# Scale alone on the way into the QKV projection; root and shift on the way out

## The chip, the core and the metric

The kernel runs on one core of a Trainium2 chip. A core has a matrix engine (TensorE, in the profile PE, with PEld for its weight loads), VectorE (DVE), ScalarE (ACT), GpSimd (POOL) and SyncE (SP), which issues the transfers. SBUF holds 128 partitions; PE writes its sums to PSUM. The metric is the device time of one execution in microseconds (us), from start to end.

## The reference

Two layers over 512 latent tokens and 256 context tokens of 1024 features: layer 0 mixes by grouped-query attention (16 query heads, 4 key and value heads of 64), layer 1 by a bidirectional state-space mixer, and each is followed by a gated convolutional feed-forward. All is float32. The change concerns the input of the attention:

```python
mod_l = jnp.split((silu_c @ ada_w[i] + ada_b[i])[:, None, :], 6, axis=-1)
mod_c = jnp.split(silu_cc @ ada_w[i] + ada_b[i], 6, axis=-1)
h_l = modulate(rms_norm(x, norm_mix_w[i]), mod_l[0], mod_l[1])   # x*rsqrt(mean x^2)*g*(1+scale)+shift
h_c = modulate(rms_norm(ctx, norm_mix_w[i]), mod_c[0], mod_c[1])
...
q_l, k_l, v_l = jnp.split(h_lat @ w_qkv, [Q_DIM, Q_DIM + KV_DIM], axis=-1)
q_l = rms_norm(q_l.reshape(bsz, seq, N_HEADS, HEAD_DIM), q_norm)
k_l = rms_norm(k_l.reshape(bsz, seq, N_KV_HEADS, HEAD_DIM), k_norm)
```

The root of a token is one number for the token; scale and shift are vectors over the features, one pair for all latents and one for the context.

## The kernel before

Data lies with features on the partitions: X holds eight tiles of 128 features x 768 tokens (512 latents, then 256 context). A float32 operand of a product is split into a rounded part and a remainder (`hi` and `lo`, `wh` and `wl`), and a product is the sum of three: hi by wh, lo by wh, hi by wl (`mm3`, L99 to L108). The casts (L85) run on ScalarE, the remainders (L87) on VectorE, in the opening also on GpSimd.

**The opening** is written out by hand in its order for PE, ScalarE and VectorE (`manual_schedule` in `attention`). SP's transfers are issued in the order of the program: first the latents of X (four loads of two feature tiles each), the parameters `par` (128 x 548), then per k-step m the weights of the modulation (`adaA`, 1 MB in three pieces), a slab of projection weights (`wslab`, 128 x 768: six groups of 128 columns) and, ahead of the rest of the slabs, the context.

1. ScalarE squares the eight latent tiles (L574), VectorE adds them up (L576), PE sums over the features (`ssa`, L274), and the root is made of it (`rstd_rows`, L265 on) and turned into a row over all partitions (`rsT`, L292). Meanwhile PE runs products of ones that nobody reads (`busy`, tile `warm`, L568).
2. SiLU of the condition (L584 on); `ada` makes the modulation of feature tile m: eight products (`ps_ada`, L128), a copy out of PSUM on VectorE (`ada_sb`, L130), two transposing products (`ps_adt`, L134), and `modulation` (L140 on), which adds the bias and makes `moda`, gain times (1 + scale).
3. `modulated` (L315) makes the operand of the products: VectorE multiplies X by `moda` and the root (`ht`, L321), ScalarE adds the shift and rounds (`hha`, L330), VectorE takes the remainder (L331).
4. Eight k-steps (m = 0 to 7): six groups of three 128x512 products into six PSUM sums (`ps_l`) kept open throughout. Beside them run the modulation and operands of the next step, in m = 1 and 2 the squares of the context (L615, L617), in m = 4 to 7 the operands of the context (`modulated` with `pool=True`, which leaves the remainder to GpSimd, L326 to L328).

**The rest of the projection** is ordered by the framework's scheduler, which respects marked orders. The six latent sums are copied to `raw` (L646); six groups of context sums `ps_c` follow (24 products of 128x256 each, copied at L863). `raw[0]` holds keys, `raw[1]` and on queries. `normed` (L668 on) makes the per-head norm and the rotary positions: squares (`qsq`, L671), gain (L672), four transfers that swap partitions (`qsw`, L675), sums on PE (`ssq`, L680), then VectorE and ScalarE up to the split into `qh` and `ql`. `values` (L654) makes six tiles of 128 tokens (24 products `ps_v` each, L660), four of latents and then two of context, and copies them out (L662). Then begins the loop over eight pairs of heads: the maxima of the scores (`ps_m`, reduced by VectorE at L768), the scores, the exponentials and the outputs. For pairs 4 to 7 the queries are projected inside this loop (`q_units`, L730 on; `ps_q`, copied by ScalarE at L738).

Of the kernel before, what the change touches and what calls it, by code (L numbers as in the profile page):

```python
# [7 lines left out]
P = 128  # L8
# [7 lines left out]
D = 1024  # L16
# [13 lines left out]
_n = 0  # L30
# [22 lines left out]
_col("cc", 2 * KT)  # L53
_col("qn", 1)
_col("kn", 1)
# [55 lines left out]
def ada(g, src, layer, chunks, m0, nm, big=True):  # L111


    nc = g.nc
    cols = nm * len(chunks) * P
    per = (1024 if big else T) // cols
    st = []
    for k0 in range(0, KT, per):
        n = min(per, KT - k0)
        t = t4(g, "wada") if big else t3(g, "wada")  # L120
        t = t[:, : n * cols].rearrange("p (k a b) -> p k a b", k=n, a=len(chunks))
        nc.sync.dma_start(t.rearrange("p k a b -> p (k a b)"), src[:, k0 * cols : (k0 + n) * cols])
        st += [t[:, k].rearrange("p a b -> p (a b)") for k in range(n)]
    yield 0
    ps = Bank(g, "ps_ada")
    for k in range(KT):
        j = k % 4
        nc.tensor.matmul(ps[32 * j : 32 * j + 32, 0:cols], g.sc32[:, k, :], st[k], start=k < 4, stop=k >= 4)  # L128
    sb = g.t3p.tile([P, 512], F32, tag="t2", bufs=6, name="ada_sb")
    nc.vector.tensor_copy(sb[:, 0:cols], ps[:, 0:cols])  # L130
    yield BREAK
    pt = Bank(g, "ps_adt")
    for i in range(cols // P):
        nc.tensor.matmul(pt[:, 2 * i : 2 * i + 2], sb[:, i * P : (i + 1) * P], g.sel, start=True, stop=True)  # L134
# [130 lines left out]
def rstd_rows(g, sq, n, cols, width, name, bank, behind=lambda: None):  # L265
# [17 lines left out]
    nc.vector.scalar_tensor_tensor(u, y, -0.5, u, ALU.mult, ALU.mult)  # L283
    rb = t3(g, f"rb{name}", n=n)
# [230 lines left out]
def attention(g, adas, project, X):  # L515
# [6 lines left out]
    g.h = [[htiles(g, n, f"a{i}_{m}") for m in range(KT)] for i, n in enumerate((L, C))]  # L522
    hl, hc = g.h
# [5 lines left out]
    mods = [ada(g, I["adaA"][m], 0, (0, 1), m, 1, big=False) for m in range(KT)]  # L529
# [12 lines left out]
    def slab():  # L542

        k = len(slabs)
        slabs.append(None)
        st = t4(g, "wst")[:, :W6]
        nc.sync.dma_start(st, I["wslab"][k])
        yield
        slabs[k] = hi, lo = slab_tile("wsh"), slab_tile("wsl")
        split(g, st, hi, lo, lo_engine="pool" if k < 7 else "dve")  # L550
# [19 lines left out]
    busy(38)  # L570
    acc = t3(g, "acc", n=L)
    for m in range(KT):
        sq = t2("sql") if m else acc
        nc.scalar.activation(sq, xs[0][m], AF.Square)  # L574
# [8 lines left out]
    e = g.p.tile([P, 2 * KT], F32, name="silu")  # L583
# [5 lines left out]
    next(norm)  # L589
# [7 lines left out]
    rs_ps, rsl = rsl, t3(g, "rsl", n=L)  # L597
    nc.scalar.copy(rsl, rs_ps)
# [7 lines left out]
    for m in range(KT):  # L606
        if 1 <= m < KT - 5 + 1:
            next(mods[m + 5 - 1])
            next(loads[m + 5 - 1])
        if m == 1:  # L610
            sqc = t3(g, "sqc", n=C)
        if m in (1, 2):
            for a in range(4 * m - 4, 4 * m):
                sq = t2("sqc")[:, :C] if a else sqc
                nc.scalar.activation(sq, xs[1][a], AF.Square)  # L615
                if a:
                    nc.vector.tensor_tensor(sqc, sqc, sq, ALU.add)  # L617
        if m == 3:
            norm = rstd_rows(g, sqc, C, g.ones[:, :1], D, "a", Bk)
            next(norm)  # L620
        if m == 4:
            rsc = t3(g, "rsc", n=C)
            pt, _, _ = next(norm)
            nc.scalar.copy(rsc, pt[:, :C])
        for j in range(6):
            if m + 1 < KT and j == 0:
                next(mods[m + 1])
            k_step(m, j, pl[j], hl)
            if m + 1 < KT:
                if j == 0:  # L630
                    next(loads[m + 1], None)
                if j == 0 + 1:
                    next(mods[m + 1])
                    modulated(g, hl[m + 1], xs[0], rsl, 0, L, 0, 1, 0, 0, m + 1)
            if m >= 4 and j == 1:
                for a in (2 * m - 8, 2 * m - 7):
                    modulated(g, hc[a], xs[1], rsc, 0, C, 0, 1, 0, 1, a, pool=True)
# [7 lines left out]
    for j in range(6):  # L645
        nc.scalar.copy(raw[j][:, :L], pl[j])  # L646
    wv = []
# [3 lines left out]

    def values():
        for t in range(T // P):
            h, c0 = (hl, t * P) if t < 4 else (hc, t * P - L)  # L654
# [7 lines left out]
            nc.scalar.copy(vt[t], ps[:, :256])  # L662
# [66 lines left out]

    def q_units(p):  # L730
        qraw[p] = qs = t3(g, "qs")
        for h, c0, n in ((hc, L, C), (hl, 0, L)):
# [5 lines left out]
            nc.scalar.copy(qs[:, c0 : c0 + n], ps[:, :n])  # L738
# [120 lines left out]
    for n, j in enumerate((0, 1, 2, 4, 5, 3)):  # L859
        ps = Bk("ps_c")  # L860
        for k in range(KT):
            k_step(k, j, ps[:, :C], hc)
        nc.scalar.copy(raw[j][:, L:], ps[:, :C])  # L863
        if n in (1, 3):
            wv.append(load_w(g, I["wv"][len(wv)], pin=True))
# [261 lines left out]
def ssd(g, x, norm, wf, close):  # L1127
# [331 lines left out]
    xn = [[g.p.tile([P, C], F32, tag="h256", bufs=16, name=f"x{m}{i}") for i in range(2)] for m in range(KT)]  # L1459
# [91 lines left out]
def body(nc, tc, I, out, dbg=None):  # L1551
# [181 lines left out]
```

## Time and profile before

| | |
|---|---|
| time of three executions | 1885.97, 1887.44, 1888.54 us; median 1887.44 us |
| the profiled execution | 1889.8 us, of it span 1888.0 us |
| TensorE clock granted, mean | 0.995 |
| instructions in the span | 27471 |
| ps_l, values and maxima begin at | 18.26, 89.19 and 96.31 us |

The profile is of one execution; the median is of others. A span runs from the first to the last instruction of the core. Engines work beside each other, so the busy times don't add up. The rows of a timeline begin with the start and the duration; a bracket at the end says how long the engine idled before and which instruction released it. The rows of groups give count, then busy time and mean nanoseconds of one, then idle time. Rows of the profile name a tile's write first and what it reads behind the arrow.

### The profile page before, as it was taken

Reading aid. Unit: us, or ns where it says so; the run is one execution under the profiler, and the core shown is the slowest. Engines: PE = TensorE matmul, PEld = TensorE weight load, DVE = VectorE, ACT = ScalarE, POOL = GpSimd, SP = SyncE. Lnnn points to the kernel's source line nnn. Section 1 sums busy time; section 2 is a strip of 40 time slices with the busy share of each in tenths; the row PEclk is TensorE's granted clock in tenths of the full one; section 3 lists DMA queues with packets and bytes.
Section 4 is the critical chain, followed back from the end, with each engine's and each line's share of the span. In section 5 each row is a group of like instructions: output and inputs, shape, how many; then the busy total and the mean of one; then the engine's idle time right before and its main releaser. Section 6 shows DMA issues by size and latency. Waiting matters only on the chain.

```text
span 1888.0 us, 27471 instructions
## 1 busy us (share of the span) xinstructions
PE 1862.3 (99%) x10794; PEld 1535.3 (81%) x10794; DVE 1346.3 (71%) x2013; ACT 832.8 (44%) x1422; POOL 251.8 (13%) x220
## 2 busy tenths in 40 slices
PE   9999999999999999999999999999999999999999
PEld 7865555689888888888898888888887888888887
DVE  5688899678777777444478977777888576565655
ACT  3655544354122222222256677766667352323331
POOL 2100000030000000000030435454434200000000
PEclk9999999989999999999999999999999999999999
DMA  9223241024443555222223344343344323323232
GB/s 342 68 83 114 89 145 62 2 78 145 156 124 121 171 188 167 68 68 67 80 77 106 91 123 133 104 133 123 108 129 136 97 74 105 101 83 107 90 101 90
DMA packets 73489, 210.02 MB, mean 111 GB/s; under 512 B 8976, under 2 KB 14480, under 8 KB 73232
## 3 DMA queue, kind: packets, MB, share of 16 engines
q1 hardware_dynamic: 73360, 208.26, 34.8%
q8 instruction: 85, 1.39, 0.3%
q14 instruction: 44, 0.36, 0.1%
HBM read 198.79 MB, written 6.82 MB: 109 GB/s over the span
## 4 chain that ended last, share of the span: by engine, by line
PE 84%; DVE 7%; DMA 3%; ACT 3%; issue 2%; SPq 1%; POOL 1%; DVEq 0%; POOLq 0%; ACTq 0%
PE ps_up L104 10%; PE ps_up L105 10%; PE ps_up L107 10%; PE ps_d L104 6%; PE ps_d L107 6%; PE ps_d L105 6%; PE ps_in L104 4%; PE ps_in L105 4%; PE ps_in L107 4%; PE ps_o L802 2%; PE ps_s L838 2%; PE ps_st L1348 1%; PE ps_wo L105 1%; PE ps_wo L107 1%; PE ps_wo L104 1%
## 5 line engine op out<-in xcount | busy, mean ns | idle before, releaser
L87 DVE TENSOR_TENSOR wl<-wst,wh 128x1024 fp32r<-128x1024 f32 x207 | 256.8, 1241 | 276.8 <-PE ps_up L105 114.2
L85 ACT CAST wh<-wst 128x1024 fp32r<-128x1024 f32 x207 | 216.9, 1048 | 440.6 <-DMA wst<-in_wup 319.5
L105 PE MATMUL ps_up<-hlf,wh 128*128 128x512 f32 x992 | 351.6, 354 | 0.0
L107 PE MATMUL ps_up<-hhf,wl 128*128 128x512 f32 x992 | 351.4, 354 | 0.0
L104 PE MATMUL ps_up<-hhf,wh 128*128 128x512 f32 x992 | 351.2, 355 | 0.0
L104 PEld LDWEIGHTS ps_up<-hhf,wh 128*128 128x128 f32 x992 | 187.5, 189 | 26.2
L105 PEld LDWEIGHTS ps_up<-hlf,wh 128*128 128x128 f32 x992 | 187.6, 189 | 26.1
L107 PEld LDWEIGHTS ps_up<-hhf,wl 128*128 128x128 f32 x992 | 187.4, 189 | 26.1
L104 PE MATMUL ps_in<-hhs,wh 128*128 128x512 f32 (+1 forms) x544 | 199.2, 366 | 0.5 <-ACT raw L1214 0.5
L107 PE MATMUL ps_in<-hhs,wl 128*128 128x512 f32 (+1 forms) x544 | 193.7, 356 | 0.0
L105 PE MATMUL ps_in<-hls,wh 128*128 128x512 f32 (+1 forms) x544 | 193.6, 356 | 0.0
L107 PE MATMUL ps_d<-hdh,wl 128*128 128x512 f32 (+1 forms) x496 | 173.4, 350 | 0.0
L104 PE MATMUL ps_d<-hdh,wh 128*128 128x512 f32 (+1 forms) x496 | 173.3, 350 | 0.1
L105 PE MATMUL ps_d<-hdl,wh 128*128 128x512 f32 (+1 forms) x496 | 172.9, 349 | 0.0
L1030 DVE SCALAR_TENSOR_TENSOR X<-ps_d,mod,X 128x256 f32<-128x256 f32 (+1 forms) x176 | 102.5, 612 | 27.1 <-PE ps_d L107 26.8
L104 PEld LDWEIGHTS ps_in<-hhs,wh 128*128 128x128 f32 x544 | 102.8, 189 | 15.3 <-issue 1.0
L107 PEld LDWEIGHTS ps_in<-hhs,wl 128*128 128x128 f32 x544 | 102.7, 189 | 14.8
L105 PEld LDWEIGHTS ps_in<-hls,wh 128*128 128x128 f32 x544 | 102.9, 189 | 13.0
L105 PEld LDWEIGHTS ps_d<-hdl,wh 128*128 128x128 f32 x496 | 93.2, 188 | 14.4 <-DVE hdl L87 0.2
L107 PEld LDWEIGHTS ps_d<-hdh,wl 128*128 128x128 f32 x496 | 93.2, 188 | 13.1
L104 PEld LDWEIGHTS ps_d<-hdh,wh 128*128 128x128 f32 x496 | 93.0, 188 | 12.9 <-ACT hdh L85 0.3
L167 DVE SCALAR_TENSOR_TENSOR junk<-wada,cb 128x1024 f32<-128x1024 f32 x80 | 97.2, 1215 | 1.0 <-ACT cb L158 0.8
(389 smaller groups left out, 3668.1 us busy)
## 6 DMA issues: line engine op xcount, KB each, us to landing
wst<-in_wup SPq DMA_DIRECT2D x88, 512.0 KB, 3.6
wada<-in_adaT SPq DMA_DIRECT2D x56, 512.0 KB, 3.6
wst<-in_win SPq DMA_DIRECT2D x48, 512.0 KB, 3.6
wst<-in_wdown SPq DMA_DIRECT2D x44, 512.0 KB, 3.7
E<-ad SPq DMA_DIRECT2D x64, 256.0 KB, 6.8
wada<-in_adaB SPq DMA_DIRECT2D x24, 512.0 KB, 4.6
ec<-ead SPq DMA_DIRECT2D x64, 128.0 KB, 4.3
wst<-in_wout SPq DMA_DIRECT2D x16, 512.0 KB, 3.6
```

Source lines behind the costliest of these rows:

```text
L85: keep(nc.scalar.copy(hi, src))
L87: keep(eng.tensor_tensor(lo, src, _r(hi), ALU.subtract))
L104: mm(out, wh, ah, start=first, stop=False)
L105: mm(out, wh, al, start=False, stop=False)
L107: i = mm(out, wl, ah, start=False, stop=last)
L167: g.tc.keep_in_program_order(nc.vector.scalar_tensor_tensor(junk, w, 1.0, cb[:, v * D : (v + 1) * D], ALU.mult, ALU.mult, accum_out=md[:, ...
L802: nc.tensor.matmul(po[S64[e], :n], v, pr[:, 512 * e + off : 512 * e + off + n], start=first, stop=last)
L838: nc.tensor.matmul(outs[e], a[S64[e], k], b[S64[e], q], start=i == 0, stop=False)
L1030: nc.vector.scalar_tensor_tensor(ap, o[:, c0:c1], gate[:, m, v : v + 1], ap, ALU.mult, ALU.add)
L1348: nc.tensor.matmul(ps[:, d * 256 : (d + 1) * 256], Bt[:, t * P : (t + 1) * P], xw[d][t], start=t == ts[0], stop=t == ts[-1])
```

## The change

The operand of a latent becomes x times `moda` alone. With r the root of a token, W the weights and s the shift, (x moda r + s) W = r (x moda W) + s W, so r is multiplied in when a sum is taken out of PSUM, and s W is added there. s W comes for keys and queries from two further columns of the context's operand tile (256 + 2 = 258 = `WX`), which hold the shift, split into hi and lo like the rest; for the values from a row `sv` that VectorE makes of the weights (`shift_row`) and that PE sums over the partitions by a product with ones (`ps_sv`). The context keeps its operands as they were. In detail:

- X comes in one load per k-step, behind the modulation's weights of the step, and no longer first of all; of `par`, the first 74 columns come behind the first piece of step 0's weights, the rest behind the last slab.
- The squares of the latents move from ahead of step 0 into steps 1 to 5, their sums and root into steps 6 and 7; the context's squares move to steps 2 and 3, its root to 4 and 5, its operands to 5, 6 and 7. Before the first latent product there are 14 + 2 + 6 warm products, not 38 + 8 + 3. Step 0 does first all groups' products hi by wh, then hi by wl, then lo by wh.
- The copies L646 and the latent half of L738 become VectorE multiplications by the root's row (`rsl`); a ScalarE bias and a two-column copy (`shift_col`) follow.
- The values are made in the order context, then latents; the latents' copies become VectorE operations with the root (`rsv`) and `sv`. The loaded weights of the values (`wvf`) are kept until `shift_row` has read them.
- hi and lo of a context operand lie in one tile of twice 258 columns. The same pool serves tiles of layer 1.

```diff
+    def scaled(m):
+        gain = g.moda[0][1][:, m, 0:1]
+        hi, lo = hr[m]
+        nc.scalar.activation(hi, xs[0][m], AF.Identity, scale=gain)
+        nc.vector.scalar_tensor_tensor(lo, xs[0][m], gain, _r(hi), ALU.mult, ALU.subtract)
...
-    busy(38)
-    acc = t3(g, "acc", n=L)
-    for m in range(KT):
-        sq = t2("sql") if m else acc
-        nc.scalar.activation(sq, xs[0][m], AF.Square)
-        if m:
-            nc.vector.tensor_tensor(acc, acc, sq, ALU.add)
-    norm = rstd_rows(g, acc, L, g.ones[:, :1], D, "a", Bk)
...
+    busy(14)
     next(mods[0])
-    busy(8)
-    rsl, _, _ = next(norm)
+    busy(2)
     next(mods[0])
     next(loads[0], None)
-    busy(3)
-    modulated(g, hl[0], xs[0], rsl, 0, L, 0, 1, 0, 0, 0)
+    scaled(0)
+    busy(6)
...
+    first_step(wh0, ah0, range(6), True)
+    next(mods[1])
+    next(loads[1], None)
+    first_step(wl0, ah0, range(4))
+    next(mods[1])
+    scaled(1)
+    shifts(0, 0)
+    first_step(wl0, ah0, range(4, 6))
+    first_step(wh0, al0, range(6))
...
+    lat = {1: (0, 1), 2: (2,), 3: (3,), 4: (4, 5), 5: (6, 7)}
...
     for j in range(6):
-        nc.scalar.copy(raw[j][:, :L], pl[j])
+        nc.vector.tensor_tensor(raw[j][:, :L], pl[j], rsl, ALU.mult)
...
+    def shift_row():
+        for k in range(KT):
+            w = wvf[k // 4][:, (k % 4) * 256 : (k % 4 + 1) * 256]
+            sh = g.mod[0][0][:, k, 0:1]
+            if k:
+                nc.vector.scalar_tensor_tensor(sv, w, sh, sv, ALU.mult, ALU.add)
+            else:
+                nc.vector.tensor_scalar(sv, w, sh, None, ALU.mult)
+
     def values():
-        for t in range(T // P):
+        for t in (4, 5, 0, 1, 2, 3):
...
+            if not t:
+                ps = Bk("ps_sv")
+                placed[0] = nc.tensor.matmul(ps[:, :256], g.ones, sv, start=True, stop=True)
+                nc.scalar.copy(sv, ps[:, :256])
...
-            nc.scalar.copy(vt[t], ps[:, :256])
+            if t < 4:
+                nc.vector.scalar_tensor_tensor(vt[t], ps[:, :256], rsv[:, t : t + 1], sv, ALU.mult, ALU.add)
+            else:
+                nc.scalar.copy(vt[t], ps[:, :256])
...
         for k in range(KT):
-            k_step(k, j, ps[:, :C], hc)
+            k_step(k, j, ps[:, :WX], hc)
         nc.scalar.copy(raw[j][:, L:], ps[:, :C])
+        nc.scalar.activation(raw[j][:, :L], raw[j][:, :L], AF.Identity, bias=shift_col(ps))
...
+        if n == 5:
+            shift_row()
```

What stands in a row on PE at the program's start, before (`ssa` are the latents' sums of squares, `rsTa` the root's row):

```order
L568 MATMUL warm<-ones 128x128 x38
L274 MATMUL ssa<-ones,acc 128x1 x4
L128 MATMUL ps_ada<-wada,sc_83 32x256 x8
L568 MATMUL warm<-ones 128x128 x8
L292 MATMUL rsTa<-cst,rba 128x128 x4
L134 MATMUL ps_adt<-cst,ada_sb 128x2 x2
L568 MATMUL warm<-ones 128x128 x3
L128 MATMUL ps_ada<-wada,sc_83 32x256 x8
L104 MATMUL ps_l<-hha_0_102,wsh 128x512
```

And after, with line numbers of the changed kernel (`hhr` and `hlr` are hi and lo of a latent operand):

```order
L590 MATMUL warm<-ones 128x128 x14
L134 MATMUL ps_ada<-wada,sc_78 32x256 x8
L590 MATMUL warm<-ones 128x128 x2
L140 MATMUL ps_adt<-cst,ada_sb 128x2 x2
L590 MATMUL warm<-ones 128x128 x6
L641 MATMUL ps_l<-hhr_97,wsh 128x512 x6
L134 MATMUL ps_ada<-wada,sc_78 32x256 x8
L641 MATMUL ps_l<-hhr_97,wsl 128x512 x4
L140 MATMUL ps_adt<-cst,ada_sb 128x2 x2
L641 MATMUL ps_l<-hhr_97,wsl 128x512 x2
L641 MATMUL ps_l<-hlr_98,wsh 128x512 x6
```

The latents' sums and root stand behind the first products now, and step 1's modulation has moved from ahead of the first product into step 0.

On VectorE, at the end of the first query and the first maxima, before (`raw_739` is the query of pair 0):

```order
L694 TENSOR_TENSOR raw_739<-raw_739,qy 128x768
L693 SCALAR_TENSOR_TENSOR qsq<-ssq,qsq 128x512
L693 SCALAR_TENSOR_TENSOR qsq<-ssq,qsq 128x256
L87 TENSOR_TENSOR wl<-wst,wh 128x1024
L695 SCALAR_TENSOR_TENSOR raw_739<-qsq,raw_739 128x768
L87 TENSOR_TENSOR ql<-raw_739,qh 128x768
L768 TENSOR_REDUCE ma<-ps_m 128x2x2
```

And after (`raw_711` is the same query):

```order
L769 TENSOR_TENSOR raw_711<-raw_711,qy 128x768
L768 SCALAR_TENSOR_TENSOR qsq<-ssq,qsq 128x512
L768 SCALAR_TENSOR_TENSOR qsq<-ssq,qsq 128x256
L770 SCALAR_TENSOR_TENSOR raw_711<-qsq,raw_711 128x768
L91 TENSOR_TENSOR ql<-raw_711,qh 128x768
L718 TENSOR_SCALAR sv<-wst,mod_81 128x256
L716 SCALAR_TENSOR_TENSOR sv<-wst,mod_81,sv 128x256 x7
L853 TENSOR_REDUCE ma<-ps_m 128x2x2
```

The eight operations of `shift_row` stand between the split of the query and the first reduction of the maxima.

On PE the values stood before as 60 products `ps_v` in a row with the first maxima behind them, and the rest of `ps_v` among these. After, where the context's two tiles end and the latents' begin:

```order
L732 MATMUL ps_v<-wl,hhc_120 128x256
L732 MATMUL ps_v<-wh,hhc_120 128x256
L725 MATMUL ps_sv<-sv,ones 128x256
L732 MATMUL ps_v<-wh,hhr_97 128x256
L732 MATMUL ps_v<-wl,hhr_97 128x256
L732 MATMUL ps_v<-wh,hlr_98 128x256
```

48 products `ps_v` stand ahead of `ps_sv` (`hhc` is a context operand), then 12 more, then the first maxima.

More of the change, by code (lines that the diff above doesn't have):

```diff
@@ L108, in mm3, with ada @@
     return i
[L111 removed]
+def ada(g, src, layer, chunks, m0, nm, big=True, also=lambda: None):
     nc = g.nc
@@ L528, in attention @@
     man.__enter__()
-    mods = [ada(g, I["adaA"][m], 0, (0, 1), m, 1, big=False) for m in range(KT)]
+    first_par = lambda: nc.sync.dma_start(g.par[:, :NFIRST], I["par"][:, :NFIRST])
+    mods = [ada(g, I["adaA"][m], 0, (0, 1), m, 1, big=False, also=(lambda: None) if m else first_par) for m in range(KT)]
     W6 = 6 * P
@@ L604, in k_step, with first_step @@
         mm3(g, tuple(w[:, ks] for w in slabs[m]), [(out, h[m])], m == 0, m == KT - 1)
[L606 to L620, printed above, removed]
+    (wh0, wl0), (ah0, al0) = slabs[0], hr[0]
+    def first_step(w, h, js, first=False):
+        for j in js:
+            nc.tensor.matmul(pl[j], w[:, j * P : (j + 1) * P], h, start=first, stop=False)
+    first_step(wh0, ah0, range(6), True)
[7 more added lines that the diff above has]
+    first_step(wh0, al0, range(6))
+    acc, sqc = t3(g, "acc", n=L), t3(g, "sqc", n=C)
+    rsv = g.p.tile([P, L // P], F32, tag="rsv", bufs=1, name="rsv")
+    lat = {1: (0, 1), 2: (2,), 3: (3,), 4: (4, 5), 5: (6, 7)}
+    rows = {}
+    for m in range(1, KT):
+        if m < 4:
+            begin(m + 4)
         if m == 4:
-            rsc = t3(g, "rsc", n=C)
-            pt, _, _ = next(norm)
-            nc.scalar.copy(rsc, pt[:, :C])
+            nc.sync.dma_start(g.par[:, NFIRST:], I["par"][:, NFIRST:])
         for j in range(6):
@@ L627, in attention @@
                 next(mods[m + 1])
[L628 to L632, printed above, removed]
-                    next(mods[m + 1])
[L634 to L637, printed above, removed]
+            k_step(m, j, pl[j], hr)
+            if m + 1 < KT and j == 0:
+                next(loads[m + 1], None)
+            if j == 1:
+                if m + 1 < KT:
+                    next(mods[m + 1])
+                    scaled(m + 1)
+                shifts(m - 1, 1)
+                shifts(m, 0)
+            if j == 2:
+                for a in lat.get(m, ()):
+                    squared(acc, xs[0][a], a)
+                if m in (2, 3):
+                    for a in range(4 * m - 8, 4 * m - 4):
+                        squared(sqc, xs[1][a], a)
+                if m == 4:
+                    rows["c"] = rstd_rows(g, sqc, C, g.ones[:, :1], D, "a", Bk)
+                    next(rows["c"])
+                if m == 5:
+                    rsc = t3(g, "rsc", n=C)
+                    nc.scalar.copy(rsc, next(rows["c"])[0][:, :C])
+                if m == 6:
+                    rows["l"] = rstd_rows(g, acc, L, g.ones[:, :1], D, "a", Bk, col=rsv)
+                    next(rows["l"])
+                if m == 7:
+                    rsl = t3(g, "rsl", n=L)
+                    nc.scalar.copy(rsl, next(rows["l"])[0])
+            if j == 3:
+                for a in {5: (0, 1), 6: (2, 3, 4), 7: (5, 6, 7)}.get(m, ()):
+                    modulated(g, tuple(t[:, :C] for t in hc[a]), xs[1], rsc, 0, C, 0, 1, 0, 1, a, pool=True)
+    shifts(KT - 1, 1)
     for _ in mods:
@@ L1456, in ssd @@
         prev = cur
-    xn = [[g.p.tile([P, C], F32, tag="h256", bufs=16, name=f"x{m}{i}") for i in range(2)] for m in range(KT)]
+    xn = [[t[:, :C], t[:, C : 2 * C]] for t in (g.p.tile([P, 2 * WX], F32, tag=f"h{C}", bufs=8, name=f"x{m}") for m in range(KT))]
     for m in range(KT):
```

100 lines of the change are left out of this document (69 added, 31 removed).

## The prediction

> **What bounds the kernel now.** First comes the page's table of busy times, then the chain of work that ended last, by engine.
>
> ```profile
> PE 1862.3 (99%) x10794; PEld 1535.3 (81%) x10794; DVE 1346.3 (71%) x2013; ACT 832.8 (44%) x1422; POOL 251.8 (13%) x220
> PE 84%; DVE 7%; DMA 3%; ACT 3%; issue 2%; SPq 1%; POOL 1%; DVEq 0%; POOLq 0%; ACTq 0%
> ```
>
> PE, the matrix engine, is the bound, and 16% of the chain lies elsewhere. The change edits the opening and the QKV projection, so the second view is the timeline of the first 100 us: where does PE wait, and for whom?
>
> ```profile
> 1.05 10.20 PE L568 MATMUL warm<-ones 128*128 128x128 f32 x76 [1.05 <-DVE ones L1575]
> 17.49 0.72 ACT L330 ACTIVATE hha<-ht,mod 128x512 fp32r<-128x512 f32 x1 [3.11 <-DVE ht L321]
> 18.26 0.50 PE L104 MATMUL ps_l<-hha,wsh 128*128 128x512 f32 x1 [0.28 <-ACT hha L330]
> 24.65 0.50 PE L104 MATMUL ps_l<-hha,wsh 128*128 128x512 f32 x1
> 34.00 0.61 PE L134 MATMUL ps_adt<-cst,ada_sb 128*128 128x2 f32 x4 [1.31 <-DVE ada_sb L130]
> 71.57 0.37 ACT L863 COPY raw<-ps_c 128x256 f32<-128x256 f32 x1
> 89.19 7.19 PE ps_v L660 x60
> 95.45 0.96 DVE L87 TENSOR_TENSOR ql<-raw,qh 128x768 fp32r<-128x768 f32 x1 [0.90 <-ACT qh L85]
> 96.31 0.50 PE L764 MATMUL ps_m<-kh,qh 64*128 64x256 f32 x4
> ```
>
> PE idles or makes warm products that compute nothing until 18.26, since the first latent operand needs squares, a root and the modulation. From there it hardly stops. The values (89.19) are followed by the maxima (96.31), whose query operand qh is ready less than 1 us before: the chain through the query of pair 0 has no slack. The table of windows gives the granted clock of some stretches.
>
> ```profile
> core 0: us, PE busy (x) PEld busy (x) DVE busy (x) ACT busy (x) POOL busy (x), PEclk, DMA share, GB/s
> 0.00:3.40 3.40, 2.35 (x11) 2.35 (x12) 0.45 (x3) 1.58 (x2) 0.20 (x4) 1.00 0.39 99
> 3.40:6.80 3.40, 3.40 (x29) 3.40 (x29) 0.85 (x2) 1.97 (x4) 0.00 (x0) 1.00 1.04 396
> 18.26:64.43 46.17, 43.91 (x264) 31.55 (x264) 25.33 (x59) 17.50 (x34) 13.97 (x10) 0.96 0.58 219
> 64.43:89.19 24.76, 23.86 (x173) 20.57 (x174) 13.95 (x20) 19.23 (x35) 2.98 (x4) 1.00 0.38 115
> 31.43:34.85 3.42, 2.11 (x12) 1.49 (x11) 2.62 (x5) 0.00 (x0) 1.83 (x1) 1.00 1.02 401
> 34.85:38.26 3.41, 3.41 (x10) 2.63 (x9) 1.69 (x4) 0.73 (x1) 0.00 (x0) 0.50 1.02 395
> 38.26:41.67 3.41, 3.41 (x30) 2.46 (x29) 1.24 (x5) 1.13 (x3) 0.81 (x1) 1.00 1.05 401
> 222.58:225.99 3.41, 2.65 (x16) 1.60 (x17) 3.41 (x4) 0.60 (x1) 0.00 (x0) 1.00 0.66 195
> 225.99:229.40 3.41, 3.41 (x15) 2.46 (x15) 2.24 (x4) 1.20 (x2) 0.00 (x0) 0.50 0.26 87
> 112.34:260.00 147.66, 143.10 (x899) 78.87 (x898) 128.37 (x180) 83.23 (x113) 0.00 (x0) 0.99 0.36 113
> ```
>
> The clock moves in steps of 3.41 us. After a window in which PE was busy for 2.11 or 2.65 us, the next runs at 0.50; the window at 34.85, wholly busy, is followed by 1.00. Half a clock is dear:
>
> ```profile
> 36.00 0.63 PE L105 MATMUL ps_l<-hla,wsh 128*128 128x512 f32 x1
> 36.43 0.63 PE L107 MATMUL ps_l<-hha,wsl 128*128 128x512 f32 x1
> 22.39 0.39 PE L105 MATMUL ps_l<-hla,wsh 128*128 128x512 f32 x1
> 22.62 0.40 PE L107 MATMUL ps_l<-hha,wsl 128*128 128x512 f32 x1
> ```
>
> Products start 0.43 us apart there, 0.23 at full rate: a slow stretch loses 0.20/0.43 = 0.46 of its length, 1.6 us for a window. One profiled execution (1889.8 us, 1888.0 of it span) carries all this; it stands 2.4 above the median 1887.44.
>
> **The change part by part.** *1. The first product.* Squares, root and shift leave its path. What remains: the first weights of the modulation, SiLU, one modulation product, its transposition, one ScalarE pass.
>
> ```profile
> 4.64 0.63 ACT L574 ACTIVATE acc<-X 128x512 f32<-128x512 f32 x1 [2.32 <-DMA X<-in_xT]
> 8.99 1.15 ACT L574 ACTIVATE sql<-X 128x512 f32<-128x512 f32 x2 [0.23 <-DMA X<-in_xT]
> 12.38 1.07 PE L128 MATMUL ps_ada<-wada,sc 128*32 128x256 f32 x16
> ```
>
> The four 512 KB loads of X end waits from 4.64 to 8.99: 1.45 us each, so the stream starts in effect at 3.2. The change loads 1.05 MB of modulation weights, parameters, 0.1 MB of constants, slab 0 (0.39 MB) and the first X (0.26 MB) in this order. At 2.8 us a MB the weights are in at 6.2 and X at some 8.2. The modulation product ends near 7.0; its PSUM copy, transposition and two VectorE steps bring me to 8.5; ScalarE's pass (0.72, as at 17.49) ends at 9.25. First product: **9.4** instead of 18.26. Between it and the second k-step lie the 6.39 us of before and one more modulation product (1.07), which stood ahead of 18.26 before: second step at 9.4 + 6.39 + 1.07 = 16.9, or 17.0 with a short wait for the second set of weights, against 24.65: **−7.65**. The spread squares cost nothing if ScalarE (17.50 of 46.17 us busy) and VectorE (25.33) hide them; uncovered, eight at 0.63 would be 5.0.
>
> *2. Waits of the k-steps.* The one at 34.00 comes of VectorE's PSUM copy standing behind four additions of squares:
>
> ```profile
> 30.18 3.43 DVE L617 TENSOR_TENSOR sqc<-sqc 128x256 f32<-128x256 f32 x4
> ```
>
> PE is idle for 46.17 − 43.91 = 2.26 us between 18.26 and 64.43 (1.31 of it here) and for 24.76 − 23.86 = 0.90 from there to the values. I let all of it go, since additions and context operands are spread and made earlier, and with the wait at 34.00 its window at half clock (1.6): −4.8. Added: the latents' sum of squares and transposed roots move into the run of products (1.0: the eight passes of L274 and four of L292 that stood before 18.26 took 1.05 and 0.60, partly beside each other); two copies of the modulation again stand behind additions (0.4, a third of 1.31); the first sum for the norm of the keys waits longer, since two bias passes, 2 × 0.59 by the L646 row below, and a small copy stand ahead of its square on ScalarE (1.4). −4.8 + 1.0 + 0.4 + 1.4 = −2.0. With part 1 the values start **9.6** earlier. Bounds: −4.9, if only part 1's gain holds and the 2.8 comes on top, and −12.4, if none of the 2.8 shows.
>
> *3. The shift's row.* It is the new wait. The values of latents t = 0 wait for ps_sv, a product of ones with sv, and sv is the last of eight dependent VectorE operations that stand behind ql on VectorE's order (shown above). Behind ps_sv on PE stand the 12 products of t = 0's first half and then the maxima, so nothing passes it.
>
> ```profile
> 73.89 2.51 SPq L675 DMA_DIRECT2D qsw<-raw  x4
> 94.59 0.83 ACT L85 CAST qh<-raw 128x768 fp32r<-128x768 f32 x1 [1.95 <-DVE raw L695]
> L321 DVE SCALAR_TENSOR_TENSOR ht<-X,moda,rsc 128x256 f32<-128x256 f32 x8 | 3.4, 479 | 0.0
> L646 ACT COPY raw<-ps_l 128x512 f32<-128x512 f32 x6 | 3.3, 590 | 0.0
> L813 DVE TENSOR_TENSOR o<-ps_o,y 128x512 f32<-128x512 f32 x8 | 5.5, 685 | 0.6 <-ACT y L812 0.5
> ```
>
> From the copy of the first context group (71.57) to the end of ql (96.41) it is 24.8 us before. Bias passes also stand ahead of the keys' transfers of qsw on the way there: +1.4 by the same price. The row itself is 8 × 0.48 = 3.8 (a dependent operation may take 0.63, as L617's do over a wait: 5.0). So sv is ready 30.0 after the copy. PE gets there after 89.19 − 71.57 = 17.6 us less 0.6 of waits that go, and 48 of 60 steps of the values, 0.8 × 7.19 = 5.8: 22.8. **+7.2**, bounds 5 and 9 by the sizes just named, and nothing at all if the row's rank on VectorE does not bind (rival 1). ps_sv itself is one full-precision product: between 0.13 (1.07/8) and 0.47 (four passes of 0.117, from 29 in 3.40); I take **0.4**.
>
> *4. The clock after it.* 7.2 us hold at least one wholly idle window. Then half rate lasts until a window was busy throughout: half a window on average and a whole one, 5.1 us at 0.46 = **+2.3**, bounds 1.6 and 3.1 (one window, two). The Trainium skill, "TensorE: Matmul & The Clock Gate", Part 1, has half rate after at least one idle window of about 3.4 us and full rate after a busy one. This trace agrees in the step (3.41 us), but by its rows a partly idle window is enough; for this wait both give the same 2.3.
>
> *5. Evacuations.* Six L646 copies go to VectorE with a factor (0.69 by L813 instead of 0.59) while PE is in ps_c, hidden. Four latent values become VectorE operations beside the maxima: **+0.4** on PE, bounds 0 and 2 (four of 0.48). In pairs 4 to 7 a query copy becomes a VectorE multiplication (0.69), a two-column copy (0.16 by a guess from the 128x4 copy below) and a ScalarE bias: VectorE gets 4 × 0.85 = 3.4 us more in a stretch where it is 128.37 of 147.66 busy.
>
> ```profile
> L772 DVE COPY mb<-ma 128x4 f32<-128x4 f32 x2 | 0.3, 165 | 0.0
> L104 PE MATMUL ps_first<-xa,wh 128*128 128x258 f32 x16 | 4.7, 292 | 0.0
> L104 PE MATMUL ps_first<-hhf,wh 128*128 128x256 f32 x40 | 11.4, 288 | 0.1
> ```
>
> I put a third of it on the path, **+1.3**; bounds 3.4, and −1.6 if the half window at 225.99 falls away. 258 columns instead of 256 cost 4 ns by these rows: nothing. The order of all engines after the attention is the same: nothing.
>
> Sum: −9.6 + 7.2 + 0.4 + 2.3 + 0.4 + 1.3 = **+2.0**: 1891.8 in a profiled execution, 1889.4 beside the median.
>
> **The rivals.** *1. The row is hidden.* The 24.8 us of the chain were measured with PE's sums for the norms and the transfers in between. If it gets 7 us shorter where these come earlier, wait and clock (9.5) vanish: −7.5, **1879.9**. For it: 1.95 and 0.90 us of waiting ahead of qh and ql alone. Against it: both rows name VectorE and ScalarE as releasers, not PE or a transfer.
> *2. VectorE bounds the pairs (slower).* The window at 222.58, with VectorE busy for 3.41 of 3.41 and PE for 2.65, shows how it goes: each further such window costs 1.6 of clock. If all 3.4 us come onto the path it is +2.1 on my sum, and if one window more tips, 1.6 on top: **1891.5 to 1893.1**. It decides from the point where VectorE has no idle time left around a pair; 87% on average speaks for a third rather than all.
> *3. The start stays cold.* Passes go 11 in the 2.35 us up to 3.40 and 29 in the next 3.40: the start is slow too. 14 warm products (28 passes) end at 5.65; then PE has products only in pieces until 9.4. By the rows, a window at 6.8 with some 80% of work (2.65 of 3.41 is 78%) is followed by half rate: 5.1 us at 0.46, +2.3, **1891.7**. By the skill's rule, which asks for a wholly idle window, this rival would not come about. I give it about an eighth, since the 80% is itself an estimate and lies at the edge.
> *4. The start doesn't move as said.* Transfers run at 396 GB/s already at 3.40; if the first set lands 3 us later, **1892.4**.
>
> **How the numbers follow.** Forecast 0.44, rival 1 0.21, rival 2 0.16, rival 3 0.13, rival 4 0.06. A measurement of this kernel tells 0.2%, 3.8 us, from no change: faster is under 1883.7, slower over 1891.2. The forecast's own spread is 1884 to 1894 (the −12.4 of part 2 and the 5 of part 3 on one side, 9, 3.1 and part 2's −4.9 on the other, never all at once): 0.03 faster, 0.33 same, 0.08 slower. Rival 1 is faster (0.20 of 0.21); rival 2 slower (0.14 of 0.16); rival 3 0.05 same, 0.08 slower; rival 4 slower (0.05 of 0.06). So 0.23, 0.42, 0.35. The range goes down to 1880, which leaves out half of rival 1, and up to 1894.5, which leaves out the most unfavourable sums: 0.18 outside.
>
> **What would show it.** The first latent product at 9 to 10 us and the second k-step at 17 (rival 4: 3 later). Granted clock 1.00 between 7 and 15 us (rival 3: 0.50). Values starting near 79. ps_sv idle before it by 5 to 9 us, released by sv's last operation, and the window behind it at 0.50 (rival 1: no idle time, clock 1.00). Between 112 and 260 the sum of PE's idle time and of half-clock windows as before or a window more (rival 2). I am wrong if ps_sv doesn't wait, or if the time after attention changes by more than 2 us.

## The result

The changed kernel takes 1899.62 us (median of six runs, 1896.67 to 1901.75) against 1887.36 us before (six runs, 1885.97 to 1888.54): a ratio of 1.0065, 95% interval 1.0052 to 1.0078. It is slower, and lies above the range of 1880 to 1894.5. The profiled execution took 1900.94 us with a span of 1899.1 us, 11.1 us more than the span of before; the forecast for this difference was +2.0.

The page of the changed kernel, its busy times and its chain by engine:

```profile
PE 1860.5 (98%) x10742; PEld 1530.3 (81%) x10742; DVE 1354.8 (71%) x2047; ACT 834.4 (44%) x1427; POOL 252.3 (13%) x219
PE 78%; DVE 10%; issue 4%; ACT 3%; DMA 3%; POOL 2%; SPq 0%; DVEq 0%; POOLq 0%; ACTq 0%
```

PE is busy for 1.8 us less than before, in a span that is 11.1 us longer: it idles for 12.9 us more, and VectorE's share of the chain grew from 7% to 10%. The timeline of PE, at the places that the prediction named:

```profile
10.68 1.65 PE L641 MATMUL ps_l<-hhr,wsh 128*128 128x512 f32 x6
17.71 0.50 PE L108 MATMUL ps_l<-hhr,wsh 128*128 128x512 f32 x1
39.42 0.61 PE L140 MATMUL ps_adt<-cst,ada_sb 128*128 128x2 f32 x4 [2.25 <-DVE ada_sb L136]
88.72 0.43 PE L732 MATMUL ps_v<-wh,hhc 128*128 128x256 f32 x1 [3.61 <-DVE wb L807]
99.43 1.22 PE L725 MATMUL ps_sv<-sv,ones 128*128 128x256 f32 x2 [3.28 <-DVE sv L716]
102.88 0.50 PE L849 MATMUL ps_m<-kh,qh 64*128 64x256 f32 x4
```

Set against the same points of before:

| begins (us) | before | after | difference |
|---|---|---|---|
| first latent product | 18.26 | 10.68 | −7.58 |
| second k-step | 24.65 | 17.71 | −6.94 |
| twelfth product of the context sums | 69.28 | 63.51 | −5.77 |
| values | 89.03 | 88.72 | −0.31 |
| first maxima | 96.31 | 102.88 | +6.57 |
| output projection, ps_dn | 378.44 | 384.79 | +6.35 |
| end of the span | 1888.0 | 1899.1 | +11.1 |

(Before, eleven products of the context sums stand among the last of the latents'; from the twelfth on the same work is done on both sides. The first product of the values begins at 89.03; the 89.19 given ahead of the prediction is the start of a piece of the chain.) So 7.3 of the 7.6 us won at the start are gone before the values, most of it in the context sums; the values lose 6.9; the loop over the pairs of heads is as long as before; and the stretch behind the attention, where hardly a line was edited, loses 4.7. The windows around the three long waits (2.25, 3.61 and 3.28 us), by the granted clock:

```profile
core 0: us, PE busy (x) PEld busy (x) DVE busy (x) ACT busy (x) POOL busy (x), PEclk, DMA share, GB/s
37.66:41.07 3.41, 1.65 (x12) 1.52 (x12) 2.10 (x5) 0.54 (x1) 1.09 (x1) 1.00 1.04 397
41.07:44.48 3.41, 3.41 (x9) 2.74 (x10) 2.52 (x8) 2.15 (x7) 0.00 (x0) 0.50 1.04 399
85.44:88.85 3.41, 0.13 (x1) 0.16 (x2) 3.32 (x7) 3.35 (x7) 0.00 (x0) 1.00 0.00 0
88.85:92.27 3.42, 3.42 (x17) 3.42 (x18) 3.39 (x5) 1.95 (x3) 0.00 (x0) 0.50 0.37 104
95.68:99.09 3.41, 0.47 (x5) 0.26 (x3) 3.16 (x8) 2.05 (x3) 0.00 (x0) 1.00 0.21 59
99.09:102.50 3.41, 3.07 (x12) 2.89 (x13) 0.29 (x1) 0.37 (x1) 0.00 (x0) 0.50 0.55 179
```

Each wait is followed by one window at half rate, some 1.6 us of loss each. Who lets PE wait is seen in VectorE's timeline:

```profile
35.61 3.42 DVE L621 TENSOR_TENSOR sqc<-sqc,sq 128x256 f32<-128x256 f32 x4
38.96 0.41 DVE L136 COPY ada_sb<-ps_ada 128x256 f32<-128x256 f32 x1
...
85.61 2.89 DVE L784 TENSOR_TENSOR kl<-raw,kh 64x768 fp32r<-64x768 f32 x3
88.42 0.21 DVE L807 COPY wb<-ps_c 128x2 f32<-128x2 f32 x2
...
94.50 0.96 DVE L91 TENSOR_TENSOR ql<-raw,qh 128x768 fp32r<-128x768 f32 x1 [1.82 <-ACT qh L89]
95.38 0.35 DVE L718 TENSOR_SCALAR sv<-wst,mod 128x256 f32<-128x256 f32 x1
95.77 3.61 DVE L716 SCALAR_TENSOR_TENSOR sv<-wst,mod,sv 128x256 f32<-128x256 f32 x7
```

At 39 the copy of the modulation out of PSUM stands behind four additions of the context's squares, as at 34 before (and behind one of the latents' at 35.01). At 88 two tiny copies (`wb`, the shift's columns of the last context sums) are the last readers of those sums' banks; they stand behind three remainders of the keys, and the first product of the values needs such a bank. At 95 the eight operations of the shift's row follow the query's split, as the order showed.

Behind the attention, the products ps_d alone, in a window of the last feed-forward, first before:

```profile
1540.00:1861.00 321.00, 110.85 (x478) 89.79 (x479) 68.29 (x158) 1.00 0.31 97
```

and after:

```profile
1540.00:1861.00 321.00, 102.30 (x432) 80.99 (x432) 62.73 (x144) 1.00 0.32 97
```

PE is busy for 110.85/478 = 0.2319 us with each before and for 102.30/432 = 0.2368 after. This counts in the end of the last product of each run, so it lies a little above the step from start to start, which the expectations below go by: 0.2292 and 0.2334 us. The same products got 2% dearer, at a full clock and a DMA share that is hardly changed.

### The profile page after: what moved, and what is told of

Its sections match the earlier page's. It is cut to its first block, busy times and chain, and to the rows that moved or that the text cites. A ratio compares the mean times of both kernels' runs of the same rounds, so it can differ in the third digit from the quotient of the medians.

```text
span 1899.1 us, 27397 instructions
## 1 busy us (share of the span) xinstructions
PE 1860.5 (98%) x10742; PEld 1530.3 (81%) x10742; DVE 1354.8 (71%) x2047; ACT 834.4 (44%) x1427; POOL 252.3 (13%) x219
## 4 chain that ended last, share of the span: by engine, by line
PE 78%; DVE 10%; issue 4%; ACT 3%; DMA 3%; POOL 2%; SPq 0%; DVEq 0%; POOLq 0%; ACTq 0%
PE ps_up L111 10%; PE ps_up L108 10%; PE ps_up L109 10%; PE ps_d L108 6%; PE ps_d L109 6%; PE ps_d L111 6%; PE ps_in L108 3%; PE ps_in L109 3%; PE ps_in L111 3%; PE ps_o L887 2%; PE ps_s L923 1%; PE ps_wo L109 1%; PE ps_wo L111 1%; PE ps_wo L108 1%; DVE xf L1312 1%
## 5 line engine op out<-in xcount | busy, mean ns | idle before, releaser
L109 PE MATMUL ps_up<-hlf,wh 128*128 128x512 f32 x664 | 258.7, 390 | 0.0
L109 PEld LDWEIGHTS ps_up<-hlf,wh 128*128 128x128 f32 x664 | 124.6, 188 | 25.0
L109 PE MATMUL ps_in<-hls,wh 128*128 128x512 f32 x368 | 143.7, 391 | 0.0
L1122 DVE SCALAR_TENSOR_TENSOR x<-ps_d,mod,x 128x256 f32<-128x256 f32 x176 | 77.1, 479 | 26.6 <-PE ps_d L111 26.3
```

What stands on the lines that cost most here:

```text
L109: mm(out, wh, al, start=False, stop=False)
L1122: nc.vector.scalar_tensor_tensor(ap, o[:, c0:c1], gate[:, m, v : v + 1], ap, ALU.mult, ALU.add)
```

## The experiments

Ratios are to the kernel before, run beside it on the same chip; the changed kernel has 1.0065.

**1. Addresses alone.** The change makes the pool of 256-column operands 256 bytes a partition larger (tiles of 2 × 258 columns) and drops and adds two small ones, so that X and all scratch behind it lie 224 bytes higher. The kernel before, shifted in the same way:

```diff
     hl, hc = g.h
+    pad = g.p.tile([P, 64], F32, name="pad")
...
-    e = g.p.tile([P, 2 * KT], F32, name="silu")
+    e = pad[:, : 2 * KT]
+    g.p.tile([P, 4], F32, tag="rsv", bufs=1, name="rsv")
```

> The kernel before with 256 unused bytes a partition behind the pool of 256-column operands, so that every tile behind it lies at the addresses that the change gives it; nothing else moves. Theory A (addresses): the 4.7 us that the changed kernel loses after 400 us come of where tiles lie. Then the products ps_d of the last feed-forward stand 0.2334 us apart as after the change, not 0.2292 as before, the stretch behind the attention is 4 to 5 us longer, and the ratio to the kernel before is 1.002 to 1.003. Rival B (it is the execution, or the weights' transfers and queues, which the earlier opening shifts): 0.2292 and a ratio of 0.999 to 1.001.

Measured: 1.0023 (1.0013 to 1.0033); the same window of ps_d alone:

```profile
1540.00:1861.00 321.00, 111.01 (x470) 88.18 (x471) 67.12 (x155) 1.00 0.31 97
```

111.01/470 = 0.2362, and up to the output projection this kernel stands where before stands (378.33 us against 378.44). Theory A holds: no instruction was moved, and by the ratio 4.4 us are lost (2.5 to 6.2 by its interval).

**2. The bank's copy on ScalarE.**

```diff
-    def shift_col(ps):
+    def shift_col(ps, copy=nc.vector.tensor_copy):
...
-        nc.vector.tensor_copy(b, ps[:, C:WX])
+        copy(b, ps[:, C:WX])
...
-        ...bias=shift_col(ps))
+        ...bias=shift_col(ps, nc.scalar.copy))
```

> After, with the two-column copy that frees a context sum's bank (shift_col in the loop of ps_c) on ScalarE, not VectorE. The first product of the values waits 3.6 us for that copy, which stands behind the remainders of the keys on VectorE. Theory A (one chain): VectorE's chain to the end of sv sets when the values of the latents go on; the wait at the start of the values goes, the wait of ps_sv grows from 3.3 to about 7 us, and at most one window at half clock (1.6 us) is gained: a median of 1898 to 1900. Rival B (two waits of their own): ps_sv still waits about 3.3 us, and 3.6 + 1.6 = 5.2 us are gained: about 1894.5.

Measured: 1.0045 (1.0029 to 1.0060). The wait at the start of the values is gone; on PE's timeline the next one has taken it over:

```profile
99.24 1.19 PE L725 MATMUL ps_sv<-sv,ones 128*128 128x256 f32 x2 [6.89 <-DVE sv L716]
102.92 0.79 PE L849 MATMUL ps_m<-kh,qh 64*128 64x256 f32 x4
```

6.89 = 3.61 + 3.28, and the maxima begin at 102.92 against 102.88: theory A, one chain through VectorE, of which the bank's wait hides a part. (This execution came to the context sums 1.6 us later, 63.79 against 62.17, with 6.8 us at half clock at 39.5 instead of 3.4; so the repair is worth about that 1.6, the window that A allows.) The median, 1896.39 us, lies below theory A's 1898 to 1900 and above rival B's 1894.5, and the ratio's interval overlaps that of the change: the wait in the trace decides here, not the time.

**3. The shift's row on GpSimd.**

```diff
-                nc.vector.scalar_tensor_tensor(sv, w, sh, sv, ALU.mult, ALU.add)
+                u = t2("svu")[:, :256]
+                nc.gpsimd.tensor_scalar(u, w, sh, None, ALU.mult)
+                nc.gpsimd.tensor_tensor(sv, sv, u, ALU.add)
```

with the first piece on GpSimd too, and each half called behind the split of its weights.

> After, with the shift's row made by GpSimd (a multiplication and an addition for each of the eight pieces, 15 operations), each half as soon as its weights are there, not by VectorE behind the split of the first query. Theory A: ps_sv waits for VectorE's rank; its wait of 3.3 us and the window at half clock behind it go, 4.9 us: about 1894.7; the wait for the bank at the start of the values (3.6 us) stays. Rival B: the maxima of pair 0 wait in its place, since their query operand isn't ready, or GpSimd's row is as late: 1898 to 1900.

Measured: 1.0047 (1.0030 to 1.0064), 1895.92 us.

```profile
82.22 2.83 PE L757 MATMUL ssq<-qsq,ones 64*64 64x512 f32 x8 [6.43 <-ACT qsq L748]
100.87 0.60 PE L727 MATMUL ps_sv<-sv,ones 128*128 128x256 f32 x2
```

ps_sv waits for nothing, as theory A says, but a wait of 6.43 us has come up ahead of the values: the query's squares are late on ScalarE. The edit also changed what the scheduler laid around it and took tiles from a pool that the query's transfers use, so this run doesn't tell the two theories apart; experiments 5 and 6 do.

**4. The opening's copies on ScalarE.**

```diff
-    nc.vector.tensor_copy(sb[:, 0:cols], ps[:, 0:cols])
+    (copy or nc.vector.tensor_copy)(sb[:, 0:cols], ps[:, 0:cols])
```

with `copy=nc.scalar.copy` for the eight of the opening.

> After, with the opening's copies of the modulation out of PSUM (ada_sb) on ScalarE, not VectorE, where they stand behind the additions of squares. Theory A: the wait of 2.25 us at 39.4 and its window at half clock (1.6) go, and since the keys' chain starts with the first context sum, the gain of 3.9 us lasts to the end: about 1895.7. Rival B: the chain behind the context sums is bound by something that doesn't start earlier (the loads of the values' weights), and the gain is taken back by longer waits at the values: 1899 to 1900.

Measured: 1.0050 (1.0036 to 1.0063), 1896.54 us. The two largest waits of the k-steps are now

```profile
39.47 0.58 PE L280 MATMUL ssa<-ones,sqc 128*128 128x1 f32 x4 [0.92 <-DVE mod L151]
51.90 0.61 PE L140 MATMUL ps_adt<-cst,ada_sb 128*128 128x2 f32 x4 [1.01 <-ACT ada_sb L136]
```

0.92 and 1.01 instead of 2.25, and no window at half clock there. The values begin at 87.05 and the maxima at 101.22, 1.7 us earlier than after: what is won ahead of the context sums lasts, but 1.9 of the expected 3.9 us went into new waits. Between the two forecasts; the interval overlaps that of the change, so this reading, too, rests on the trace.

**5. The shift's row on PE.** No VectorE operation is left in it:

```diff
-                placed[0] = nc.tensor.matmul(ps[:, :256], g.ones, sv, start=True, stop=True)
+                for k in range(KT):
+                    sh = g.mod[0][0][:, k, 0:1].broadcast_to([P, P])
+                    placed[0] = nc.tensor.matmul(ps[:, :256], sh, wvf[k // 4][:, (k % 4) * 256 : (k % 4 + 1) * 256],
+                                                 start=k == 0, stop=k == KT - 1)
...
-        if n == 5:
-            shift_row()
```

> After, with the shift's row summed by PE alone: eight full-precision products of the weights with a column of the shift read 128 times over (stride 0) take the place of the eight VectorE operations and the one product with ones. Nothing waits for VectorE there any more. Theory A (one chain behind VectorE): the wait of 3.3 us ahead of ps_sv and its half-clock window (1.6) go, some 2 us of products come: about 3 us less than after, 1896.5; the values' first wait, for the bank, stays at 3.6. Rival B: the maxima wait for their query instead, and nothing is gained.

Measured: 1.0048 (1.0031 to 1.0064), 1895.18 us.

```profile
90.31 0.36 PE L735 MATMUL ps_v<-wh,hhc 128*128 128x256 f32 x1 [3.61 <-DVE wb L810]
97.57 3.62 PE L727 MATMUL ps_sv<-wst,mod 128*128 128x256 f32 x16
```

The wait ahead of ps_sv is gone, the bank's is unchanged. The eight products take 3.6 us, not the 2 I had put (0.45 us each, near the 0.47 that the prediction has as the upper bound of one), which eats most of the gain: the maxima begin at 102.54, 0.3 us earlier than after, or 1.9 if one counts that this execution, too, came to the context sums 1.6 us late (63.77).

**6. Both.** Experiments 2 and 5 together.

> The row on PE and the bank's copy on ScalarE together. Theory A: with the end of the chain off the path the bank's wait is worth its own price; both waits and both half windows go (3.6 + 3.3 + 3.2), 2 us of products come: about 8 us less than after, 1891.5, and the first maxima at 94 to 95 us, where the query's operand (ready near 94.4) may hold them for up to 1 us. Rival B: the maxima wait for the query's chain for as long as the two waits were together, about 1896.

Measured: 1.0008 (0.9997 to 1.0020), 1888.63 us.

```profile
90.37 3.62 PE L727 MATMUL ps_sv<-wst,mod 128*128 128x256 f32 x16
95.34 0.50 PE L852 MATMUL ps_m<-kh,qh 64*128 64x256 f32 x4
```

The values begin at 84.57, the maxima at 95.34, 7.5 us earlier than after, without a wait. This execution reached the context sums at 61.96, as after did. Alone the repairs were worth 1.6 and 1.9 us up to the maxima, together 7.5. The median is 2.9 us under theory A's 1891.5, and rival B's 1896 is out. The two waits were one chain, VectorE's, seen at two places, and only where its end is off the path does the bank's wait count in full.

**7. Which address.** The kernel before, with 224 unused bytes between the weight tiles and X, so that X and the scratch move and the weights don't; one run (1889.74 us), as the step of the products is read from the trace.

```diff
-    e = g.p.tile([P, 2 * KT], F32, name="silu")
+    pad = g.p.tile([P, 72], F32, name="silu")
+    e = pad[:, : 2 * KT]
```

> The kernel before with 224 unused bytes between the weight tiles and X: X, the scratch of the attention and of the feed-forwards (the moving operands of ps_d) move by 224 bytes, the weight tiles don't. If the place of the moving operand sets the step of ps_d, the products of the last feed-forward stand 0.2334 us apart as in the first shifted kernel; if the place of the weights does, 0.2292.

```profile
1540.00:1861.00 321.00, 112.83 (x478) 89.64 (x479) 68.34 (x158) 1.00 0.31 97
```

112.83/478 = 0.2360, as in experiment 1: for this shift the weights' place has no part in it. What moved of ps_d's operands is the moving one, hi and lo of the feed-forward's inner values.

**8. Another shift.** Before, with 96 bytes instead of 256 (`g.p.tile([P, 24], F32, name="pad")` behind the operands), weights and scratch both.

> The kernel before with 96 unused bytes behind the 256-column operands: everything behind them moves by 96 bytes. If only 224 or 256 bytes are bad by their own (the offset within some period), ps_d stands at 0.2292 or lower; if any shift is worse, near 0.2334.

Measured in one run: 1902.76 us, where the kernel before took 1886.29 (median of 15). The windows of ps_d alone and of ps_up alone:

```profile
1540.00:1861.00 321.00, 100.39 (x432) 81.16 (x432) 62.51 (x144) 1.00 0.31 97
1540.00:1861.00 321.00, 223.54 (x949) 178.51 (x948) 42.95 (x59) 15.57 (x20) 1.00 0.31 97
```

and ps_up in the kernel before:

```profile
1540.00:1861.00 321.00, 213.24 (x933) 174.66 (x931) 43.63 (x60) 15.54 (x20) 1.00 0.31 97
```

ps_d has 100.39/432 = 0.2324, about as before, but ps_up 223.54/949 = 0.2356 instead of 0.2286, and there are twice as many of it. The forecast on ps_d came true, and I hadn't asked about ps_up. The moving operand of ps_up (`hhf`) didn't move here; its weights did.

**9. After, in the old place.** The small tiles of the maxima go to the end of memory and 32 unused bytes fill up, so that X and all behind it have the addresses of before.

```diff
-    small = lambda name, dt=F32: g.p.tile([P, 2, T // P], dt, tag="mx", bufs=4, name=name)
+    small = lambda name, dt=F32: g.t3p.tile([P, 2, T // P], dt, tag="mx", bufs=4, name=name)
...
     rsv = g.p.tile([P, L // P], F32, tag="rsv", bufs=1, name="rsv")
+    g.p.tile([P, 8], F32, name="pad")
```

> After with X and everything behind it at the addresses of before (the small tiles of the maxima move to the end of memory, 32 unused bytes fill the rest), and no other edit. Theory A (addresses): ps_d of the last feed-forward stands at 0.2292 us again, not 0.2334, and 4.2 us are gained: a ratio of 1.004 instead of 1.0065. Rival B: in the changed kernel the step has another reason: 0.2334, 1.0065.

Measured: 1.0041 (1.0027 to 1.0056).

```profile
1540.00:1861.00 321.00, 110.44 (x476) 89.46 (x477) 67.98 (x157) 1.00 0.32 97
```

110.44/476 = 0.2320. Theory A holds in the changed kernel too; the ratio is the 1.004 that it forecast, though its interval touches that of the change.

**10. Both waits and the old place** (experiments 6 and 9 together).

> Both waits taken away as in the run before (the row on PE, the bank's copy on ScalarE), and the old place for X and all behind it. If addresses and waits add up: 4.2 us less than the 1.0008 of that run, a ratio of 0.9986.

Measured: 0.9995 (0.9985 to 1.0004), 1884.8 us. The forecast, 0.9986, lies at the edge of the interval; the parts add up roughly.

**11. And step 5's copy.** Experiment 10 with `copy=nc.scalar.copy if m == 5 else None` in the opening's `ada`, and the sum of the context's squares issued at group 4 of step 4, not group 2.

> The run before this one, and in the opening only step 5's copy of the modulation on ScalarE (the one behind the additions at 39 us), with the sum of the context's squares two groups later. Theory A: the wait of 2.4 us and its window at half clock (1.6) go and nothing takes their place: a ratio of 0.9965. Rival B: as when all eight copies moved, other waits of about 1 us appear and 2 us are gained: 0.9975.

Measured: 0.9980 (0.9971 to 0.9988), 1882.4 us: faster than both kernels. The one wait over 0.9 us left in the k-steps, and the first maxima:

```profile
44.73 0.61 PE L140 MATMUL ps_adt<-cst,ada_sb 128*128 128x2 f32 x4 [0.94 <-DVE ada_sb L136]
93.33 0.50 PE L853 MATMUL ps_m<-kh,qh 64*128 64x256 f32 x4
```

The wait moved to the copy of the next step (2.26 us became 0.94), as rival B had it. The maxima begin 3.0 us earlier than before, at 93.33 against 96.31: that is what is left on the path of the 7 us that the change wins at the start. Not all of the gain comes from there: in the profiles the first feed-forward takes 509.84 us instead of the 512.48 of before, and no experiment here explains these 2.6 us.

## Why the prediction was wrong

**The start was right, the size a little large.** Forecast −8.9 for the first product and −7.65 for the second step; measured −7.58 and −6.94. The 14 warm products took 6.18 us instead of 4.6, all at the slow rate, so the modulation product began at 7.16 and ended 1.2 us later than the forecast 7.0; the weights, in at 6.75 instead of 6.2, were there before it. The cold start (rival 3) didn't come: the window after 6.93 was busy throughout and at 1.00. Transfers (rival 4) were in time.

**The first step that failed is "I let all of it go"**, in part 2. The wait at 34.00 was put down to the place of four additions ahead of a copy on VectorE. The change puts five ahead of such a copy, in step 4 instead of step 2, and I never laid the new order beside the old one there: the wait came back at 39.42 with 2.25 instead of 1.31 us, and its half window with it. From the second k-step to the twelfth product of the context sums 1.2 us were lost, where the sum had 2.5 won (2.26 and 1.6 less 1.4). Experiment 4 shows that the copy's place behind VectorE's work is the cause: with the copy on another engine the wait shrinks and the half window goes.

What made that work so long escaped the prediction as well. The last of the four additions, on VectorE, and the remainder of the weights that GpSimd takes at the same time, first before, then after:

```profile
31.50 1.83 POOL L87 TENSOR_TENSOR wsl<-wst,wsh 128x768 fp32r<-128x768 f32 x1 [3.59 <-ACT wsh L85]
31.76 1.85 DVE L617 TENSOR_TENSOR sqc<-sqc 128x256 f32<-128x256 f32 x1
36.88 1.87 POOL L91 TENSOR_TENSOR wsl<-wst,wsh 128x768 fp32r<-128x768 f32 x1 [3.42 <-ACT wsh L89]
37.20 1.84 DVE L621 TENSOR_TENSOR sqc<-sqc,sq 128x256 f32<-128x256 f32 x1
```

Both times this addition takes 1.85 and 1.84 us, where the three ahead of it take 0.43 each, and it ends 0.28 us after GpSimd's operation. These 1.4 us are more than the whole wait of before. One step earlier in the changed kernel a copy stands behind four additions too, but GpSimd is idle, the last three are through in 1.48 us, and PE doesn't wait:

```profile
28.41 1.48 DVE L621 TENSOR_TENSOR sqc<-sqc,sq 128x256 f32<-128x256 f32 x3
29.81 0.42 DVE L136 COPY ada_sb<-ps_ada 128x256 f32<-128x256 f32 x1
```

So additions ahead of a copy cost PE little here; an addition that meets GpSimd's remainder does. No experiment moved that remainder, so this rests on the traces alone.

**The second is a bank that I didn't follow.** Part 2 counts the small copy ahead of a ScalarE pass, but not that it is the reader that frees a PSUM bank. From there to the values 5.5 us were lost, 0.5 in the sum: 3.61 of it is this wait. By experiments 2, 5 and 6 it cost little of its own, though, while the shift's row stood behind it.

**The shift's row was right as a chain, not in where PE pays for it.** Forecast: a wait of 7.2 us at ps_sv, 5 to 9, and 2.3 of clock. Measured: 3.28 there, since PE had already waited 3.61 for the bank, together 6.89, and two half windows. With the bank's wait away (experiment 2) all 6.89 stand at ps_sv. From the values' start to the maxima 14.2 us instead of 7.3 passed, 6.9 more against 9.9 in the sum (7.2, 0.4 and 2.3): a part lay in the bank's wait, which I had not in the sum, so the two misses partly cancel.

**The pairs of heads came out even by luck.** Forecast +0.4 and +1.3; measured 281.91 us from the maxima to the output projection against 282.13. But the clock differs: first before, then after, then the kernel of experiment 7, which has the instructions of before.

```profile
96.31:378.44 282.13, 276.28 (x1718) 161.33 (x1717) 238.44 (x342) 134.44 (x181) 0.00 (x0) 0.99 0.25 82
102.88:384.79 281.91, 274.35 (x1718) 160.12 (x1717) 242.24 (x353) 132.52 (x175) 0.00 (x0) 1.00 0.25 82
95.38:375.38 280.00, 274.56 (x1717) 159.95 (x1716) 238.33 (x341) 133.99 (x180) 0.00 (x0) 1.00 0.25 82
```

The half window at 225.99, worth 1.6 us, is missing after. It is missing in experiment 7 too, so its absence is no mark of the change. At an equal clock the changed kernel takes 1.9 us more here (281.91 against 280.00), with PE idle for 7.56 us instead of 5.44: the terms, 1.7 in sum, were about right, and the −1.6 that the prediction named only as a bound hid them. Rival 2, the slower one, didn't come about: no further window tipped.

**The last failed step is "the order of all engines after the attention is the same: nothing"**. The order is, the addresses aren't. By the ratios of experiments 1 and 9 they cost 0.23% and 0.24%, some 4.4 us, and experiment 7 names the moving operands. That is near the 4.7 that the profile lost there, but not in the same places. From first product to first product of the stages (us):

| stage | before | experiment 1 | after | experiment 9 |
|---|---|---|---|---|
| first feed-forward, ps_up to sss | 512.48 | 514.44 | 512.48 | 509.66 |
| mixer, ps_in to ps_wo | 417.04 | 415.25 | 419.72 | 414.84 |
| last feed-forward, ps_up to its end | 351.25 | 353.05 | 353.11 | 351.26 |

The last feed-forward loses 1.9 us with the addresses and has them back in the old place: that part is shown. In the first one the addresses cost 2.0 in the old kernel and 2.8 in the changed one, but the changed kernel is as fast as before there, so something else in it wins 2.8, which stays open. The mixer's 2.7 are waits of PE (7.07 us idle instead of 3.82), and they are this execution's: in the profiles of the experiments the stage takes 414.8 to 418.3 us. So of the 4.7 the addresses account for 1.9 by the trace.

In sum: the start, the wait that stayed and the new bank turn −9.6 into −0.3 (9.3 worse: 0.7, 3.7 and 5.0), the values are 3.0 better than their term and the pairs 1.9 (1.6 of it the missing half window), the tail is 4.7 worse: 9.1 in all, the distance between +2.0 and +11.1.

## What to carry to other kernels

When work moves between steps, look again at what then stands ahead of each small PSUM reader on its engine, since such a reader frees a bank or feeds the next product, and look at each operation's own time there, not at a mean: one of 1.84 us among three of 0.43 is a wait of its own; a wait that goes at one place is paid at the next one on the same chain, so repairs have to be tried together before one of them is called useless. A change of tile sizes moves every tile behind it in memory: before explaining a loss in an untouched stage, compare the step of its products with that of a kernel whose only edit is the shift, stage by stage. And before a stretch of equal length is called free, compare its granted clock.

## What the hardware showed that I had not expected

The step of back-to-back 128x512 products in full clock depends on where their operands lie: 0.2319 us for ps_d before, 0.2360 with only X and the scratch 224 bytes higher, 0.2324 with 96; ps_up went from 0.2286 to 0.2356 with the weights 96 bytes higher. Which property of an address decides wasn't settled, and one shift of 96 bytes cost more (16 us in its single run) than the whole change. The Trainium skill, "TensorE: Matmul & The Clock Gate", Part 1, gives 215.7 ns from start to start for 512 columns in a warm array; no run here shows it: the lowest mean busy time of one is 0.2284 (ps_up in the changed kernel, 218.81/958).

VectorE operations that read two inputs from SBUF end with GpSimd's remainder when they meet it: in the changed kernel the 128x2 operation of `moda` takes 1.51 us at 31.97 beside one that runs from 31.62 to 33.46, and 0.16 us at 40.33 beside none. The copies out of PSUM aren't held: in experiment 11 `ada_sb` takes 0.42 us at 44.25 beside a remainder from 44.28 to 46.11.

A partly idle window doesn't always bring half rate. The prediction took it as a rule from windows with PE busy for 2.11 and 2.65 us. In experiment 10 the wait at 39.47 left a window with 1.82 us of work, and the clock stayed:

```profile
35.39:38.81 3.42, 1.82 (x11) 1.05 (x6) 3.11 (x5) 1.46 (x4) 1.87 (x1) 1.00 1.03 390
38.81:42.22 3.41, 2.75 (x16) 2.46 (x17) 1.89 (x8) 1.65 (x4) 0.00 (x0) 1.00 1.04 391
```

After a window with 1.65 in the changed kernel it halved, and after one with 2.65 in the kernel before. So nearly the same wait costs 1.6 us in one execution and nothing in another, and the share of work in the window doesn't decide it; what does stays open.
